# A two-layer decoder trunk on one core: eight landing places for 48 blocks, another order for the second and third phase of a seven-product projection, and attention moved

## The chip, the cores and the metric

The kernel runs on one core of a Trainium2 chip, in one launch. The metric is the device time in microseconds; the profile is of one execution of the same program.

## The reference

Two layers act on x (256 tokens of width 2048, float32), with a memory of 256 tokens beside them. Layer 0 mixes by trailing means over 2, 4, 8 and 16 tokens, layer 1 by block attention; both have a four-head attention into the memory, SiLU gates, an output projection and a layer norm.

```
for i in range(2):
    if i == 1:
        k, v = split(h @ w_kv_shared)
    u = h @ w_in[i]
    branch_in, gate_b, mem_q, gate_m = split(u, [1536, 3072, 3584])
    branch = multiscale_pool(branch_in) if i == 0 else moba_attention(branch_in, k, v)
    mem_o = memory_attention(mem_q, mem, w_mem_kv[i])
    mixed = concat(branch * silu(gate_b), mem_o * silu(gate_m))
    h = layer_norm(ALPHA * h + mixed @ w_out[i], ln_g[i], ln_b[i])
```

## The kernel before

The whole program is one list, `items`. An item is a block of weights, 128 x 1024 values of float32 (512 KB): it is loaded by SyncE into a landing place `raw`, split into a high part `wh` (ScalarE, L73) and a low part `wl = raw - wh` (VectorE, L74), and multiplied on TensorE: high weights with high and low tokens, low weights with high tokens. `run()` walks over the list by hand: in step i it splits item i + 3, issues loads of items ahead, issues item i's products, and then runs what earlier items have put down for this step with `later(n, fn)` (n steps on). There are four buffers each of `raw`, `wh` and `wl`. The first `SHARE` items are loaded `LD0` = 8 items ahead, their landing places being the four `raw` and four pieces of a scratch tile that later becomes `res`; from there on loads go out 4 items ahead into the four `raw`. Each engine's queue runs in order; SyncE's has the loads and the DMA transposes.

An ordinary block makes twelve products of 128x512. The projections of the memory query and memory gate (columns 6 and 7 of `w_in[0]`) are made another way (class `Seven`): with tokens and weights quartered, seven products of half the size instead of eight, as in Strassen's method. Their 28 short blocks of six products each are called p1 to p7, each for the four pieces a, b, c, d: in phase A p1 and p5, in phase B p3, p7, p6 (a3, a7, a6, b3, ...), in phase C p2, p4 (a2, a4, ...). p5, p7, p6 and p4 need a sum of weight blocks first (L729, VectorE). Sums of tokens lie in `zT`. The products gather in the PSUM banks X (`pt`), Y (`o`), V and W (the halves of `s2`, printed as s). Two calls on VectorE and ScalarE make the results: `second` (L710 to L716, after phase B: rows of the memory gate, whose `done2` applies tanh, L287, and a product, L288, then planes of 16 bits, L276, and DMA transposes, L279) and `third` (after phase C: rows of the memory query). Between the short blocks stand ordinary blocks o0 to o23: o0 to o7 a gate of the pool, o8 to o15 and o16 to o23 its inputs. Their results are transposed and joined on ScalarE (L302); from the joined inputs the pool's groups are made in steps on VectorE (L774, L782, L783) and split into `zT`.

Counted from the list's start, p1 of piece a is item 30, o10 42, a3 43, a7 44, o15 54, o16 58, o17 61, o21 73 in both kernels. After item 72 `attend` puts down the memory attention of head pairs 0 and 1: `plan(pair, a, turns, b, c)` sets the step of the scores (a), of four groups of 32x32 transposes (L381), of the splits of the probabilities (b) and of the product with the values (c), counted from there. In that stretch stand the pool's mix with bank o (L822 reads it), the rest of the gates, and then the output projection.

Of the kernel before, what the change touches and what calls it, by code (L numbers as in the profile page):

```python
# [15 lines left out]
ALU = mybir.AluOpType  # L16
# [21 lines left out]
SLOTS = 7  # L38
LD = 4
LD0 = 8  # L40
SHARE = 32
FAR = 6
LP = 3
SEND = 3
# [5 lines left out]
def trunk(ctx: ExitStack, tc: tile.TileContext, a: dict, out: bass.AP):  # L50
    nc = tc.nc
# [16 lines left out]
    def mm(o, l, r, start, stop, **kw):  # L68
        nc.tensor.matmul(o, l, r, start=start, stop=stop, **kw)  # L69
# [7 lines left out]
    items = []  # L77
# [9 lines left out]
    def item(src, cols, consume=None, dst=None):  # L87
        items.append(dict(src=src, cols=cols, consume=consume, dst=dst, cuts=(0, cols)))
# [8 lines left out]
    def later(n, fn):  # L97
        events[now[0] + n].append(fn)
# [111 lines left out]
    def moving(w, src):  # L210

        if len(src.shape) == 3:
            return w.rearrange("p (c k n) -> p k c n", c=2, k=2)
        return w.rearrange("p (k n) -> p k n", n=512)
# [84 lines left out]
    def join(dst, tp, n0=0):  # L299

        n = dst.shape[1]
        nc.scalar.activation(dst.bitcast(U16).rearrange("p n (x h) -> p n h x", h=2), tp[:, n0:n0 + n], AF.Copy)  # L302
# [35 lines left out]
    def heads_tile(name):  # L338
        return sb.tile([P, 4, 2 * T], F32R, name=name)
# [152 lines left out]
    def plan(pr, a, turns, b, c):  # L492

        later(a, pr.a)
        later(a + 1, pr.exps)
        later(a + 2, pr.divide)
        for g, t in enumerate(turns):
            later(t, lambda g=g: pr.turn(g))
        later(b, lambda: pr.b(0))
        later(b + 1, lambda: pr.b(1))  # L500
        later(c, pr.c)
# [119 lines left out]
    class Seven:  # L621
# [46 lines left out]
        def project(self, n1, n2, done1, done2):  # L668
            b, held = {}, {}
            s1, s5 = (lambda: ebuf[:, 0]), (lambda: ebuf[:, 1])  # L670
            e5, e7, e6, e3 = (self.summed(n) for n in range(4))
            a11, a12, a22 = self.tokens(0, 0), self.tokens(8, 0), self.tokens(8, 1)

            def kept(q):
                nm = ("qq", "pp")[q // 2]
                if nm not in held:
                    held[nm] = sb.tile([P, 2 * BLK], F32, name=nm)
                return held[nm][:, q % 2 * BLK:(q % 2 + 1) * BLK]

            def bank(nm):  # L680
                if nm not in b:
                    if nm in "VW":
                        s = ps.tile([P, 2, 512], F32, name="s2")
                        b["V"], b["W"] = s[:, 0], s[:, 1]
                    else:
                        b[nm] = ps.tile([P, 512], F32, name={"X": "pt", "Y": "o"}[nm])
                return b[nm]

            def one(q, src, nm, sta, begin, then=None, make=None):
                def consume(wh, wl):  # L690
                    o = bank(nm)
                    h, l = (moving(w, n1[0]) for w in (wh, wl))
                    for kk in range(2):
                        xh, xl = sta(2 * q + kk)
                        mm(o, xh, h[:, kk], begin and q == kk == 0, False, skip_group_check=not begin)
                        mm(o, xl, h[:, kk], False, False, skip_group_check=not begin)
                    for kk in range(2):
                        mm(o, sta(2 * q + kk)[0], l[:, kk], False, q == 3 and kk == 1, skip_group_check=not begin)
                    if q == 3 and then:
                        then()  # L700
                item(src, BLK, consume)
                it = items.pop()
                if make:
                    it["make"] = make
                return it

            def copy(to, nm):
                return lambda: nc.scalar.activation(to(), b[nm], AF.Copy)

            def second():  # L710
                nc.vector.tensor_add(s5(), s5(), b["V"])
                nc.vector.scalar_tensor_tensor(b["W"], b["X"], -1.0, s5(), op0=ALU.mult, op1=ALU.subtract)
                nc.scalar.activation(s5(), b["X"], AF.Copy)
                nc.vector.scalar_tensor_tensor(b["Y"], b["Y"], -1.0, s5(), op0=ALU.mult, op1=ALU.subtract)
                done2(0, b["Y"])
                done2(1, b["W"])  # L716

            def third():
                nc.vector.tensor_add(b["Y"], b["Y"], s1())
                done1(0, b["Y"])  # L720
                nc.vector.tensor_add(b["V"], b["V"], s5())
                done1(1, b["V"])

            groups = [], [], []
            for q in range(4):
                def added(x, y, to=None):
                    def make(it):
                        r = to() if to else it["raw"]
                        nc.vector.tensor_add(r, x(), y(it))  # L729
                        return r  # L730
                    return make
                k = lambda q=q: kept(q)
                raw = lambda it: it["raw"]
                p1 = one(q, n1[q], "X", a11, True, copy(s1, "X"))
                p5 = one(q, n2[q], "Y", e5, True, copy(s5, "Y"),
                         added(lambda p1=p1: p1["raw"], raw, k))
                groups[0].append((p1, p5))
                p3 = one(q, n2[4 + q], "Y", e3, False)
                last = lambda it, p3=p3: p3["raw"]
                p7 = one(q, n2[q], "V", e7, True, None, added(lambda p3=p3: p3["raw"], raw))  # L740
                p6 = one(q, None, "X", e6, False, second, added(k, last, k))
                groups[1].append((p3, p7, p6))
                p2 = one(q, n1[4 + q], "Y", a12, True)
                p4 = one(q, None, "V", a22, False, third,
                         added(k, lambda it, p2=p2: p2["raw"], k))
                groups[2].append((p2, p4))
            return groups
# [39 lines left out]
    def to_pool(base, where):  # L787
        def then(t, tp, pl):
            i = base
            while i < base + 4:  # L790
                n = min(3 - i % 3, base + 4 - i)
                join((U0, U1)[i // 3 % 2][:, i % 3:i % 3 + n, PAD + t * P:PAD + (t + 1) * P], tp, i - base)
                i += n
                if t == 1 and i % 3 == 0:
                    *steps, spread = pool_group(i // 3 - 1)
                    n, by = 1 + 4 * (i == 12), 1 + (i != 6)
                    for j, fn in enumerate(steps):
                        later(n + j // by, fn)
                    later(n + (len(steps) + by - 1) // by, spread)
        return turned(where, then)  # L800
# [53 lines left out]
    def pool_in(c, where):  # L854
        return collect(proj_n, xT, cols(a["w_in"][0], c), to_pool(4 * c, where))

    def pool_gate(c, where):
        slots = [(4 * c + d + 4) % SLOTS for d in range(4)]
        return collect(proj_n, xT, cols(a["w_in"][0], 3 + c), gates(slots, where))
# [4 lines left out]
    def hooked(it, fn):  # L864

        old = it["consume"]

        def go(*w):
            if old is not None:
                old(*w)  # L870
            fn()
        it["consume"] = go
        return it
# [24 lines left out]
    o = pool_gate(0, in_p) + pool_in(0, in_p) + pool_in(1, in_pp)  # L898
# [10 lines left out]
        p1, p5 = A[q]  # L909
        items += [p1, o[6 + q], p5]  # L910
    (a3, a7, a6), (b3, b7, b6), (c3, c7, c6), (d3, d7, d6) = B
    items += [o[10], a3, a7, o[11], a6, b3, o[12], b7, o[13], b6, o[14], c3, o[15], c7, c6, d3, o[16], d7, d6]
    (a2, a4), (b2, b4), (c2, c4), (d2, d4) = C
    items += [o[17], o[18], a2, a4, b2, o[19], b4, c2, o[20], c4, d2, d4]
    hooked(items[SHARE + 1], pools)
    prs = [MemPair(h0, st, mem_gate) for h0 in (0, 2)]

    def attend(prs=prs):
        plan(prs[0], 7, (10, 11, 12, 13), 14, 20)
        plan(prs[1], 16, (19, 20, 21, 22), 24, 27)  # L920
    after(attend)
    m, g, p, h = mix(0), pool_gate(1, in_q), pool_in(2, in_q), pool_gate(2, in_q)
    items += [o[21], o[22], g[0], *m, g[1], o[23]]
# [54 lines left out]
    for grp in range(3):  # L978
        k = fresh("k", lambda: heads_tile("kk"))
        q = fresh("q", lambda: heads_tile("qq"))  # L980
# [3 lines left out]
        prs = [MobaPair(2 * j, 4 * grp + 2 * j, st) for j in range(2)]  # L984
# [52 lines left out]
    scr = sb.tile([P, 4 * BLK], F32, name="res")  # L1037
    for i in range(SHARE):
        items[i]["lead"] = LD0
# [45 lines left out]
    one = sb.tile([P, BLK], F32R, name="wh", bufs=W_BUFS)[:, :P]  # L1085
# [18 lines left out]
    o = last(0, 0, 512)  # L1104
# [5 lines left out]
    o = last(1, 0, 256)  # L1110
# [6 lines left out]
    o = last(1, 256, 512)  # L1117
# [103 lines left out]
```

## Time and profile before

| what | value |
|---|---|
| time, median of 3 runs | 816.43 us (816.1 to 817.44) |
| profiled execution | 815.97 us |
| its span | 814.2 us |
| mean granted clock of TensorE | 0.992 |
| TensorE (PE) busy | 791.6 us, 97% |
| VectorE (DVE) busy | 618.2 us, 76% |
| ScalarE (ACT) busy | 500.3 us, 61% |
| loads `raw<-in_w_in` | 127 on the page, 512 KB each, median 5.1 us to landing |

PE are the products, PEld their weight loads, which overlap them. A row of the timeline has the start and the time taken in us, the engine, the line, the operation, output <- input, the count, and in brackets the idle time before it with what ended it. A row of the waits has the total, the count and the longest. A row of a stretch has its length, then each engine's busy time, TensorE's granted clock (1.00 is full), the DMA engines' share and GB/s. In the profile the helper's line stands for all its calls, so tiles tell the calls apart.

### The profile page before, as it was taken

How to read it: one execution, taken by the hardware profiler on the slowest of the kernel's cores; microseconds unless marked ns; L12 is line 12 of the kernel's file. 1: busy time of each engine (PE TensorE's matmuls, PEld its weight loads, DVE VectorE, ACT ScalarE, POOL GpSimd, SP SyncE). 2: the span in 40 equal slices, each digit the busy share in tenths (PEclk: the TensorE clock that was granted, in tenths of full speed). 3: DMA queues.
4: the chain of work that ended last, by engine and by line, in shares of the span. 5: the costliest groups of instructions: out<-in, count | busy, mean ns of one | idle time of the engine just before them, and what ended most of it. 6: DMA issues, size and time to landing. Idle time of an engine off the chain costs nothing.

```text
span 814.2 us, 10066 instructions
## 1 busy us (share of the span) xinstructions
PE 791.6 (97%) x3634; PEld 654.5 (80%) x3634; DVE 618.2 (76%) x827; ACT 500.3 (61%) x618; POOL 0.2 (0%) x4
## 2 busy tenths in 40 slices
PE   9999898899989999999999999999999999999997
PEld 6888575678878888888888888888888888888886
DVE  5779787958987875576856796797568955988966
ACT  5667656766666554369967676466765565655531
POOL 0000000000000000000000000000000000000000
PEclk9999999899999999999999999999999999999999
DMA  8984766677666775679995577757865588657922
GB/s 318 383 280 142 216 215 192 183 206 213 178 195 181 257 280 191 199 219 269 267 262 169 175 226 226 169 182 195 235 199 176 189 217 245 179 181 247 319 86 103
DMA packets 122393, 174.25 MB, mean 214 GB/s; under 512 B 58210, under 2 KB 60258, under 8 KB 122082
## 3 DMA queue, kind: packets, MB, share of 16 engines
q1 hardware_dynamic: 121024, 170.16, 69.5%
q10 hardware_dynamic: 1320, 3.46, 1.2%
q8 instruction: 28, 0.46, 0.2%
q14 instruction: 21, 0.17, 0.1%
HBM read 158.39 MB, written 2.10 MB: 197 GB/s over the span
## 4 chain that ended last, share of the span: by engine, by line
PE 85%; ACT 5%; DVE 5%; DMA 3%; issue 3%; SPq 0%; ACTq 0%; DVEq 0%
PE acc L69 76%; PE s L69 3%; PE o L69 3%; ACT wh L73 2%; PE pt L69 2%; DMA raw<-in_w_in 2%; DVE wl L74 2%; DMA raw<-in_w_mv 1%; ACT pl L276 1%; DVE p L381 1%; ACT gate L302 0%; ACT res L302 0%; ACT zT L73 0%; SPq L115 0%; ACT zf L287 0%
## 5 line engine op out<-in xcount | busy, mean ns | idle before, releaser
L74 DVE TENSOR_TENSOR wl<-raw,wh 128x1024 fp32r<-128x1024 f32 (+3 forms) x237 | 281.4, 1200 | 114.7 <-ACT wh L73 112.8
L69 PE MATMUL acc<-wh,xm 128*128 128x512 f32 x1280 | 321.7, 391 | 0.1
L73 ACT ACTIVATE wh<-raw 128x1024 fp32r<-128x1024 f32 (+3 forms) x237 | 240.4, 1036 | 128.0 <-PE acc L69 50.5
L69 PEld LDWEIGHTS acc<-wh,xm 128*128 128x128 f32 x1280 | 240.4, 189 | 50.3 <-ACT wh L73 0.8
L69 PE MATMUL acc<-wl,xm 128*128 128x512 f32 x640 | 174.3, 389 | 0.0
L69 PEld LDWEIGHTS acc<-wl,xm 128*128 128x128 f32 x640 | 120.2, 188 | 25.0
L69 PE MATMUL acc<-wh,zT 128*128 128x512 f32 x448 | 112.0, 390 | 0.0
L69 PEld LDWEIGHTS acc<-wh,zT 128*128 128x128 f32 x448 | 83.7, 188 | 17.1
L69 PE MATMUL acc<-xm 128*128 128x512 f32 x288 | 66.3, 389 | 0.0
L381 DVE STREAM_TRANSPOSE p<-ebuf 32x192 f32<-32x192 f32 (+1 forms) x160 | 63.3, 396 | 2.4
L69 PEld LDWEIGHTS acc<-xm 128*128 128x128 f32 x288 | 53.7, 188 | 10.9
L69 PE MATMUL acc<-wl,zT 128*128 128x512 f32 x224 | 61.0, 389 | 0.0
L69 PEld LDWEIGHTS acc<-wl,zT 128*128 128x128 f32 x224 | 42.1, 188 | 8.7
L74 DVE TENSOR_TENSOR xm<-raw,xm 128x1024 fp32r<-128x1024 f32 (+2 forms) x31 | 35.4, 1154 | 9.5 <-ACT xm L73 9.1
L73 ACT ACTIVATE xm<-raw 128x1024 fp32r<-128x1024 f32 (+2 forms) x31 | 29.9, 994 | 5.8 <-PE acc L69 3.0
L73 ACT ACTIVATE pp<-p 128x384 fp32r<-128x384 f32 (+1 forms) x20 | 11.2, 560 | 31.0 <-DVE p L381 31.0
L73 ACT ACTIVATE zT<-zf 128x512 fp32r<-128x512 f32 (+1 forms) x18 | 10.5, 584 | 27.5 <-DVE zf L387 20.6
L276 ACT ACTIVATE pl<-acc 128x1024 uint16<-128x1024 uint16 x24 | 23.8, 1019 | 4.0 <-PE acc L69 4.0
L69 PE MATMUL acc<-xm,zT 128*128 128x256 f32 (+1 forms) x144 | 22.6, 318 | 0.0
L69 PEld LDWEIGHTS acc<-xm,zT 128*128 128x128 f32 x144 | 20.7, 191 | 1.9
L302 ACT ACTIVATE pl<-ln_g 128x1024 uint16<-128x1024 uint16 x14 | 19.0, 1356 | 0.0
L287 ACT ACTIVATE zf<-acc 128x512 f32<-128x512 f32 x14 | 8.2, 596 | 16.9 <-PE acc L69 16.9
(206 smaller groups left out, 679.6 us busy)
## 6 DMA issues: line engine op xcount, KB each, us to landing
raw<-in_w_in SPq DMA_DIRECT2D x127, 512.0 KB, 5.1
raw<-in_w_out SPq DMA_DIRECT2D x58, 512.0 KB, 3.9
raw<-in_w_sk SPq DMA_DIRECT2D x24, 512.0 KB, 4.3
raw<-in_w_sv SPq DMA_DIRECT2D x24, 512.0 KB, 3.9
raw<-in_w_mv SPq DMA_DIRECT2D x13, 512.0 KB, 6.0
raw<-in_w_mk SPq DMA_DIRECT2D x10, 512.0 KB, 5.3
res<-in_w_mk SPq DMA_DIRECT2D x5, 512.0 KB, 7.1
res<-in_w_in SPq DMA_DIRECT2D x5, 512.0 KB, 7.8
```

The costliest lines, as they stand in the source:

```text
L69: nc.tensor.matmul(o, l, r, start=start, stop=stop, **kw)
L73: nc.scalar.activation(hi, src, AF.Copy)
L74: nc.vector.tensor_sub(lo, src, f(hi))
L276: nc.scalar.activation(pls[0][:, t], src.bitcast(U16).rearrange("p (n h) -> p h n", h=2), AF.Copy)
L287: nc.scalar.activation(src, acc, AF.Tanh, scale=0.5)
L302: nc.scalar.activation(dst.bitcast(U16).rearrange("p n (x h) -> p n h x", h=2), tp[:, n0:n0 + n], AF.Copy)
L381: nc.vector.transpose(self.p[32 * g:32 * g + 32, h * self.n:(h + 1) * self.n], self.e[32 * h:32 * h + 32, g * self.n:(g + 1) * self.n])
```

## The change

- `SHARE` goes from 32 to 48: items 32 to 47 are loaded eight ahead into eight landing places. With it the pool's scratch (`pools`, four memsets, and the tile `res` in the landing places' memory) comes at item 49 instead of 33.
- p3 begins its bank instead of adding to p5's. `second` is cut in two. One step after the last p6, s5 becomes -X - s5 (L711 of the changed kernel). One step after the last p7, `results` takes bank Y and then V from that sum, with the gate's tanh and product behind each, and only then copies X for the third phase.
- The last pair of phase B is d6, d7 instead of d7, d6. Ahead of phase C stand o17, o18, o19 instead of o17, o18, and the order is a2, a4, b2, b4, o20, c2, c4, d2, d4 instead of a2, a4, b2, o19, b4, c2, o20, c4, d2, d4.
- The steps of the pool's first group are put four items later.
- The first pair's scores, turns and first splits come one item later, the second pair's product two items later.

```diff
-SHARE = 32
+SHARE = 48
...
             def second():
-                nc.vector.tensor_add(s5(), s5(), b["V"])
-                nc.vector.scalar_tensor_tensor(b["W"], b["X"], -1.0, s5(), op0=ALU.mult, op1=ALU.subtract)
+                nc.vector.scalar_tensor_tensor(s5(), b["X"], -1.0, s5(), op0=ALU.mult, op1=ALU.subtract)
+
+            def results():
+                nc.vector.tensor_sub(b["Y"], s5(), b["Y"])
+                done2(0, b["Y"])
+                nc.vector.tensor_sub(b["W"], s5(), b["V"])
+                done2(1, b["W"])
                 nc.scalar.activation(s5(), b["X"], AF.Copy)
-                nc.vector.scalar_tensor_tensor(b["Y"], b["Y"], -1.0, s5(), op0=ALU.mult, op1=ALU.subtract)
-                done2(0, b["Y"])
-                done2(1, b["W"])
...
-                p3 = one(q, n2[4 + q], "Y", e3, False)
+                p3 = one(q, n2[4 + q], "Y", e3, True)
...
-                p7 = one(q, n2[q], "V", e7, True, None, added(lambda p3=p3: p3["raw"], raw))
-                p6 = one(q, None, "X", e6, False, second, added(k, last, k))
+                p7 = one(q, n2[q], "V", e7, True, lambda: later(1, results), added(lambda p3=p3: p3["raw"], raw))
+                p6 = one(q, None, "X", e6, False, lambda: later(1, second), added(k, last, k))
...
-                    n, by = 1 + 4 * (i == 12), 1 + (i != 6)
+                    n, by = {3: 5, 12: 5}.get(i, 1), 1 + (i != 6)
...
-    items += [... c6, d3, o[16], d7, d6]
+    items += [... c6, d3, o[16], d6, d7]
...
-    items += [o[17], o[18], a2, a4, b2, o[19], b4, c2, o[20], c4, d2, d4]
+    items += [o[17], o[18], o[19], a2, a4, b2, b4, o[20], c2, c4, d2, d4]
...
-        plan(prs[0], 7, (10, 11, 12, 13), 14, 20)
-        plan(prs[1], 16, (19, 20, 21, 22), 24, 27)
+        plan(prs[0], 8, (11, 12, 13, 14), 15, 20)
+        plan(prs[1], 16, (19, 20, 21, 22), 24, 29)
```

SyncE's queue around items 28 to 61, first as it was. The first row are items 28 to 31, the pair on qq the transposes of the memory keys, the first pair on p those of the pool's gate, the second those of the pool's first input.

```order
L113 DMA res<-in_w_in 128x2x512 x4
L279 DMA_TRANSPOSE qq<-pl 128x8x128 x2
L113 DMA raw<-in_w_in 128x2x512 x11
L279 DMA_TRANSPOSE p<-pl 128x8x128 x2
L113 DMA raw<-in_w_in 128x2x512 x15
L279 DMA_TRANSPOSE p<-pl 128x8x128 x2
```

The first pair on p stood behind the load of o10 (item 42). Now:

```order
L113 DMA res<-in_w_in 128x2x512 x4
L113 DMA raw<-in_w_in 128x2x512
L279 DMA_TRANSPOSE qq<-pl 128x8x128 x2
L113 DMA raw<-in_w_in 128x2x512 x3
L113 DMA res<-in_w_in 128x2x512 x4
L113 DMA raw<-in_w_in 128x2x512 x4
L113 DMA res<-in_w_in 128x2x512 x2
L279 DMA_TRANSPOSE p<-pl 128x8x128 x2
L113 DMA res<-in_w_in 128x2x512
L113 DMA raw<-in_w_in 128x2x512 x11
L279 DMA_TRANSPOSE p<-pl 128x8x128 x2
```

The loads of a3, a7 and o11 have moved ahead of the first pair on p, and six of the loads ahead of it go to the scratch (res) instead of a `raw`.

VectorE's queue from the end of phase B to a4's low split, as it was (the first two rows are the low splits of o18 and a2; qq<-qq,raw is a4's sum; L774, L782 and L783 are the pool's first group):

```order
L74 TENSOR_TENSOR wl<-raw,wh 128x1024 x2
L711 TENSOR_TENSOR ebuf<-ebuf,s_822 128x512
L712 SCALAR_TENSOR_TENSOR s_822<-pt,ebuf 128x512
L714 SCALAR_TENSOR_TENSOR o<-o,ebuf 128x512
L288 SCALAR_TENSOR_TENSOR zf<-zf,o 128x512
L288 SCALAR_TENSOR_TENSOR zf<-zf,s_822 128x512
L774 TENSOR_TENSOR res<-res 128x3x256
L782 TENSOR_TENSOR res<-res,ln_g 128x3x256
L729 TENSOR_TENSOR qq<-qq,raw 128x1024
L783 TENSOR_TENSOR res<-res 128x3x256
L74 TENSOR_TENSOR wl<-raw,wh 128x1024
L74 TENSOR_TENSOR wl<-qq,wh 128x1024
```

And as it is now (the row ahead of L714 is a2's low split, the two sums qq<-qq,raw are a4's and b4's):

```order
L711 SCALAR_TENSOR_TENSOR ebuf<-pt,ebuf 128x512
L74 TENSOR_TENSOR wl<-raw,wh 128x1024
L714 TENSOR_TENSOR o<-ebuf,o 128x512
L288 SCALAR_TENSOR_TENSOR zf<-zf,o 128x512
L716 TENSOR_TENSOR s_810<-ebuf,s_810 128x512
L288 SCALAR_TENSOR_TENSOR zf<-zf,s_810 128x512
L731 TENSOR_TENSOR qq<-qq,raw 128x1024
L74 TENSOR_TENSOR wl<-raw,wh 128x1024
L74 TENSOR_TENSOR wl<-qq,wh 128x1024
L731 TENSOR_TENSOR qq<-qq,raw 128x1024
L776 TENSOR_TENSOR res<-res 128x3x256
L784 TENSOR_TENSOR res<-res,ln_g 128x3x256
```

The first result stands behind a2's split and frees bank o before the second is begun; the pool's steps have moved from ahead of a4's sum to behind b4's.

TensorE's queue at the second pair's product (o<-pp,vv), as it was: pt, o and s are the pool's second mix, acc the gate's blocks behind it.

```order
L69 MATMUL o<-zT,wh 128x256 x6
L69 MATMUL o<-zT,wl 128x256 x3
L69 MATMUL s_1924<-zT,wh 128x256 x6
L69 MATMUL s_1924<-zT,wl 128x256 x3
L69 MATMUL o<-pp,vv 128x256 x12
L69 MATMUL acc<-wh,xm 128x512 x8
```

And now:

```order
L69 MATMUL s_1917<-zT,wh 128x256 x6
L69 MATMUL s_1917<-zT,wl 128x256 x3
L69 MATMUL acc<-wh,xm 128x512 x8
L69 MATMUL acc<-wl,xm 128x512 x4
L69 MATMUL acc<-wh,xm 128x512 x8
L69 MATMUL acc<-wl,xm 128x512 x4
L69 MATMUL o<-pp,vv 128x256 x12
```

Two ordinary blocks have come between the mix and the product.

More of the change, by code (lines that the diff above doesn't have):

```diff
@@ L911, in trunk @@
     (a3, a7, a6), (b3, b7, b6), (c3, c7, c6), (d3, d7, d6) = B
-    items += [o[10], a3, a7, o[11], a6, b3, o[12], b7, o[13], b6, o[14], c3, o[15], c7, c6, d3, o[16], d7, d6]
+    items += [o[10], a3, a7, o[11], a6, b3, o[12], b7, o[13], b6, o[14], c3, o[15], c7, c6, d3, o[16], d6, d7]
     (a2, a4), (b2, b4), (c2, c4), (d2, d4) = C
-    items += [o[17], o[18], a2, a4, b2, o[19], b4, c2, o[20], c4, d2, d4]
+    items += [o[17], o[18], o[19], a2, a4, b2, b4, o[20], c2, c4, d2, d4]
     hooked(items[SHARE + 1], pools)
```

## The prediction

> **What bounds the kernel now.** I read the head of the page first, then busy time by stage, then what TensorE's weight loads (PEld) waited for.
>
> ```profile
> span 814.2 us, 10066 instructions
> PE 791.6 (97%) x3634; PEld 654.5 (80%) x3634; DVE 618.2 (76%) x827; ACT 500.3 (61%) x618; POOL 0.2 (0%) x4
> ```
>
> ```profile
> core 0: us, PE busy (x) PEld busy (x) DVE busy (x) ACT busy (x) POOL busy (x), PEclk, DMA share, GB/s
> 66.00:132.00 66.00, 61.19 (x255) 46.49 (x254) 55.31 (x56) 42.52 (x50) 0.00 (x0) 1.00 0.69 208
> 132.00:163.50 31.50, 25.59 (x97) 19.94 (x97) 26.95 (x27) 21.67 (x26) 0.00 (x0) 0.89 0.59 168
> 163.50:262.00 98.50, 94.27 (x456) 79.68 (x455) 78.47 (x113) 65.03 (x88) 0.00 (x0) 0.98 0.70 194
> 262.00:800.00 538.00, 538.00 (x2504) 450.77 (x2503) 402.37 (x562) 325.81 (x404) 0.00 (x0) 1.00 0.71 212
> 63.70:86.30 22.60, 21.51 (x94) 17.14 (x93) 22.38 (x30) 15.44 (x20) 0.00 (x0) 1.00 0.50 161
> ```
>
> TensorE is the bound: from 262 to 800 us it has no idle time, so a microsecond gained earlier reaches the end whole. What can be gained lies before: 4.8 us idle from 66 to 132, 5.9 in the next stage, 4.2 after it, and the time in which the clock was below 1.00. The last row says that VectorE is full from 63.7 to 86.3; nothing that comes earlier for it can move that stretch.
>
> The waits that follow are nearly all of short blocks (banks o, s, pt), whose weights ScalarE and VectorE have to add and split. I go through the change in the order of time.
>
> **Part 1, eight landing places.** Removed is the wait for loads; no instruction is added. These rows are of SyncE, then of the three engines.
>
> ```profile
> 82.92 4.33 SPq L279 DMA_TRANSPOSE p<-pl  x2
> 87.36 34.21 SPq L113 DMA_DIRECT2D raw<-in_w_in  x15
> ...
> 86.27 1.22 DVE L729 TENSOR_TENSOR pp<-raw 128x1024 f32<-128x1024 f32 x1
> 89.62 0.76 PEld L69 LDWEIGHTS o<-wh,zT 128*128 128x128 f32 x4 [1.11 <-ACT wh L73]
> 92.03 1.06 ACT L73 ACTIVATE wh<-raw 128x1024 fp32r<-128x1024 f32 x1 [1.98 <-DMA raw<-in_w_in]
> 98.03 0.76 PEld L69 LDWEIGHTS s<-wh,zT 128*128 128x128 f32 x4 [1.91 <-ACT wh L73]
> 106.28 2.99 ACT L73 ACTIVATE wh<-raw 128x1024 fp32r<-128x1024 f32 x3 [3.40 <-DMA raw<-in_w_in]
> ```
>
> And these are PEld's waits by cause from 105 to 127 us (the first two) and from 127 to 132.1:
>
> ```profile
> PEld s L69 <- DVE wl L74: 0.7, 1, 0.7
> PEld s L69 <- ACT wh L73: 0.4, 1, 0.4
> ...
> PEld pt L69 <- DVE wl L74: 0.9, 1, 0.9
> PEld s L69 <- DVE wl L74: 0.5, 1, 0.5
> PEld pt L69 <- ACT wh L73: 0.3, 1, 0.3
> PEld s L69 <- ACT wh L73: 0.3, 1, 0.3
> ```
>
> a3's load is the first behind the transposes of 82.92: issued at 87.36, it landed at 92.03, 4.7 us later. Now a3's, a7's and o11's loads stand ahead of the transposes. Up to 86.27 nothing moves (VectorE full). Then d's sum for p5 ends at 87.5; ScalarE is free, its split takes 1.06, and the matmul starts at 88.7 instead of 89.62. a3's split need not wait until 92.03, so a7, behind o10, a3 and two pairs of gate joins on ScalarE (1.4 us each, row of 130.00 below), starts at 95.3 instead of 98.03: 2.7 us earlier. The load waited for at 106.28 is issued some ten microseconds earlier too, which takes most of b7's waits (0.4 and 0.7): 3.5. d6 and d7 change places; of their four waits (2.0 us) I keep 0.6 for d7's low half, since VectorE does d6's split first. o17, which starts at 132.12 (row below), starts at 127.7: **4.4 us**. Bounds: nothing if VectorE's row were as full from 86 to 132 as before it (it is busy 84% from 66 to 132), and the 4.8 us that TensorE is idle there.
>
> Cover: the four loads behind the transposes (b3, o12, b7, o13) now go out in one row from 87.4 on; at the 4.7 us above and 2.5 us more for each that follows (512 KB at the stage's 208 GB/s) the last is there by 99.6, and wanted at 101 or later.
>
> **Part 2, second results, three ordinary blocks, pool steps.**
>
> ```profile
> 130.00 1.39 ACT L302 ACTIVATE res<-p 128x768 uint16<-128x768 uint16 x2
> 132.12 1.78 PEld L69 LDWEIGHTS acc<-wh,xm 128*128 128x128 f32 x8
> ...
> 135.75 0.68 DVE L711 TENSOR_TENSOR ebuf<-ebuf,s 128x512 f32<-128x512 f32 x1
> 138.63 0.60 ACT L287 ACTIVATE zf<-o 128x512 f32<-128x512 f32 x1 [0.77 <-DVE o L714]
> 139.98 2.01 ACT L276 ACTIVATE pl<-zf 128x1024 uint16<-128x1024 uint16 x2 [0.27 <-DVE zf L288]
> 140.00 0.77 PEld L69 LDWEIGHTS o<-wh,xm 128*128 128x128 f32 x4 [2.47 <-DVE zf L288]
> 140.46 0.95 DVE L774 TENSOR_TENSOR res<-res 128x768 f32<-128x768 f32 x1
> ...
> 143.64 1.06 ACT L73 ACTIVATE wh<-qq 128x1024 fp32r<-128x1024 f32 x1 [0.70 <-DVE qq L729]
> ...
> 144.74 0.76 PEld L69 LDWEIGHTS s<-wh,xm 128*128 128x128 f32 x4 [3.50 <-ACT wh L73]
> 163.53 0.64 PEld L69 LDWEIGHTS acc<-wh,xm 128*128 128x128 f32 x3
> ```
>
> Eight weight loads of an ordinary block take 1.78 us, so its twelve take 2.7 and a short block's six 1.36. From o17 (132.12) to o21 (163.53) are 31.4 us, of which four ordinary and eight short blocks are 21.8: 9.6 are lost, in a2's wait of 2.47, a4's of 3.50 and the clock behind them.
>
> The arithmetic of the results is three vector operations before and after (0.7 each), and one ScalarE copy in both, now off the path; its worth is the order. Worked forward: o17 starts at 127.7. d7's high split stands on ScalarE at 124.6; behind it come joins, o18, joins, o19, a2 (1.06 for a split, 1.4 for two joins): 7.0 us, so a2's ends at 131.6; its low split on VectorE ends near 133, and the results begin at 133.5. Subtraction 0.7, tanh 0.6, L288 0.7 and hand-offs: bank o is free at 135.7. TensorE needs it at 127.7 + 3 x 2.7 = 135.9. **a2's wait of 2.47 goes.**
>
> What is late next is a4. The second result runs to 137.0; then ScalarE has, ahead of a4's split, the copy (0.6), the two planes (the 2.01 of the row, which stood behind it before) and b2's split (1.06): a4's split is at 140.3, its matmul at 141.4, while a2 ends at 137.2. A wait of 4.2 us, no shorter than the 3.50 before. From there VectorE is the bound: a4, b2, b4 follow each other without an ordinary block to cover their sums, and the first pool group's four steps (0.95 each, moved here from ahead of a4) lie between them. From a4's low split at 141.5 to d4's there are ten operations of 1.15 to 1.2 and these four, 15.5 us; d4's low half starts at 158.3 and o21 at 158.7. That is 31.0 us from o17 against 31.4: **0.4 us**. Most of what the three blocks cover comes back as waits of a4, b4, c4 and d4. Bounds: 9.6 us if none of these waits came, and a loss of 2.4 if every sum, split and product of the four pairs ran one behind the other (1.3 + 1.1 + 1.6 + 1.36 each, with o20 24.2 from 141.4).
>
> **Part 3, attention.**
>
> ```profile
> 181.28 0.30 PEld L69 LDWEIGHTS s<-kk,qq 128*128 128x128 f32 x2 [0.92 <-ACT qq L310]
> 182.54 1.24 PEld L69 LDWEIGHTS s<-kk,qq 128*128 128x128 f32 x10 [0.96 <-DVE qq L311]
> 220.45 1.61 PEld L69 LDWEIGHTS o<-pp,vv 128*128 128x128 f32 x12
> 242.07 2.64 PEld L69 LDWEIGHTS o<-pp,vv 128*128 128x128 f32 x12 [3.15 <-issue]
> ```
>
> The first pair's scores go behind one more ordinary block, 2.7 us, against waits of 0.92 and 0.96: **1.9 us**. The second pair's last product waits 3.15 us for the bank o that the pool's mix has just filled and VectorE not yet read; moved behind two ordinary blocks (5.4 us) it finds it free. Behind that wait the same twelve loads take 2.64 us against 1.61. The clock's rows say why:
>
> ```profile
> 142.53:145.95 3.42, 1.19 (x4) 0.67 (x4) 3.42 (x4) 2.72 (x4) 0.00 (x0) 1.00 1.21 213
> 145.95:149.36 3.41, 2.62 (x6) 2.15 (x7) 3.41 (x4) 1.37 (x2) 0.00 (x0) 0.50 0.28 81
> 149.36:152.77 3.41, 3.41 (x9) 2.65 (x9) 3.34 (x4) 2.83 (x4) 0.00 (x0) 0.50 0.73 225
> 238.11:241.52 3.41, 1.01 (x9) 0.81 (x7) 2.27 (x4) 2.74 (x4) 0.00 (x0) 1.00 1.04 323
> 241.52:244.93 3.41, 2.83 (x13) 2.86 (x14) 2.89 (x6) 1.05 (x2) 0.00 (x0) 0.50 1.11 261
> ```
>
> A stretch with TensorE busy 1.0 to 1.2 us of 3.41 is followed by one or two at half the clock. So the moved product gains 3.15 + 1.03 = **4.2 us**. Its users: the gated output follows three microseconds behind it on VectorE and ScalarE, and the out projection's second block, which reads it, now stands three ordinary blocks (8.1 us) behind. Were that cover gone, it would cost one for one. The Trainium skill (TensorE: Matmul & The Clock Gate, section on the HAM clock gate) gives one idle window of about 3.4 us as what sends the clock to half. By that rule a wait of 3.15 us would have cost no clock, this term would be 3.1, and the sum's end 806.6. The row of 238.11 disagrees: it was not idle throughout, and half speed followed. The measurement decides.
>
> a4's wait of 4.2 us will bring the half clock again; I cost it at nothing, because TensorE waits for VectorE from there to o21.
>
> **Sum.** 4.4 + 0.4 + 1.9 + 4.2 = 10.9 us off the profiled execution's 815.97 (span 814.2 and 1.8 around it): 805.1. The median of the runs is 816.43, 0.46 higher; I say **805.5**. The memsets of the pool's scratch, which move by 16 items, and the later loads I cost at nothing: both are behind TensorE's ordinary blocks, and VectorE only gains room where it was full.
>
> **Rivals.**
> *The landing places bring nothing.* VectorE, full until 86.3, stays the bound, and everything up to o17 stands where it stood. For it: the 22.38 of 22.60. Against it: ScalarE's waits of 1.98 and 3.40 for loads. Without the 4.4: 809.9.
> *Phase three runs free.* VectorE makes up its row while o17 to o19 run, and b4, c4 and d4 find their splits done. Against it: VectorE was busy 27 of 31.5 us in a stage that was 31.4 long. Without these three pairs of waits (some 4.9 us): 800.6.
> *The clock stays at half.* a4's wait sends it down, and short blocks that wait for VectorE keep it there: 145.95 to 149.36 was 77% busy and did not bring it back. From a4 on TensorE's 12.2 us of work to o21 would take 24.5: o21 at 165.9, 7.2 us later than I say, end at 812.7. If it stayed low further, each two microseconds cost one more, and from about 177 us on the kernel would be slower than before; that is the way to the other side. Against it: 149.36 to 152.77 was fully busy and full speed followed, and a half clock itself raises the busy share. The Trainium skill (same page, section on HAM oscillation) describes such a kernel that falls back at each of its waits; no run here shows more than two slow stretches in a row.
>
> **How the numbers follow.** My forecast 0.72; places without effect 0.10; free phase three 0.08; clock 0.10 (half of it slower than before, some of it level). 0.2%, 1.6 us, is about what a measurement of this kernel can tell. Faster by more: 0.93; within: 0.02; slower: 0.05. The range goes from 800.5 (free phase three) to 810.0 (no effect of the places) and leaves out the clock's case and slips of several terms together, under 2 in 10.
>
> **What would show it.** Right: no wait for raw at ScalarE from 87 to 107; o17 near 127.7; no wait at a2; a wait of about four microseconds at a4, by the split of qq, then half the clock; o21 near 158.7; no wait at the scores, nor at the second pair's product, and the clock at 1.00 around it. Wrong: loads late behind the transposes, gate joins that ScalarE waits for, or a clock below 1.00 beyond o21.

## The result, and the profile after

The changed kernel takes 809.12 us (median of four runs, 807.82 to 810.55) against 816.93 (816.1 to 817.69) for the kernel before on the same chip: a ratio of 0.9905, 95% interval 0.9881 to 0.9929. A second set, six runs of it beside eleven of the kernel before, gave 809.08 against 815.37, 0.9924 (0.9908 to 0.994). So it is faster by 0.6 to 1.2%, 3.6 us behind the forecast of 805.5 and inside its range.

The page's head, and then busy time by stage as in the prediction (TensorE, its loads, VectorE, ScalarE, GpSimd, clock, DMA share, GB/s):

```profile
span 806.3 us, 10062 instructions
PE 787.4 (98%) x3634; PEld 651.8 (81%) x3634; DVE 617.7 (77%) x827; ACT 498.8 (62%) x618; POOL 0.2 (0%) x4
```

```profile
66.00:126.40 60.40, 58.87 (x253) 46.66 (x252) 54.62 (x55) 42.40 (x50) 0.00 (x0) 1.00 0.72 210
126.41:157.27 30.86, 25.22 (x98) 18.46 (x97) 25.93 (x26) 20.92 (x26) 0.00 (x0) 0.94 0.58 167
157.27:256.00 98.73, 95.52 (x469) 80.72 (x468) 80.08 (x115) 64.44 (x89) 0.00 (x0) 1.00 0.70 198
256.00:800.00 544.00, 542.50 (x2544) 454.85 (x2542) 407.85 (x577) 326.43 (x406) 0.00 (x0) 1.00 0.70 211
```

Of the 4.8 us that TensorE was idle up to o17, 1.5 are left. In the third phase it is idle for 5.6. In the third row 3.2 us are idle at full clock. The last row, full before, now has 1.5 us idle. What these idle times are say the waits of PEld from 60 to 300 us (total, count, longest):

```profile
PEld s L69 <- ACT wh L73: 6.3, 4, 4.3
PEld s L69 <- DVE wl L74: 4.2, 6, 1.6
PEld acc L69 <- DVE zf L288: 3.6, 1, 3.6
PEld o L69 <- ACT wh L73: 1.5, 2, 1.3
PEld acc L69 <- DVE zT L74: 1.1, 1, 1.1
PEld o L69 <- DVE wl L74: 1.0, 2, 0.5
```

The waits of the scores (0.9 and 1.0) and of the second pair's product (3.1) are gone. Two are new, both of blocks that gather in acc: 3.6 us for the gate's product L288, and 1.1 us for zT. The timeline of PEld at the places that the prediction named, and at the two new waits:

```profile
126.41 1.80 PEld L69 LDWEIGHTS acc<-wh,xm 128*128 128x128 f32 x8
...
134.69 0.78 PEld L69 LDWEIGHTS o<-wh,xm 128*128 128x128 f32 x4
...
140.19 1.06 PEld L69 LDWEIGHTS s<-wh,xm 128*128 128x128 f32 x4 [4.25 <-ACT wh L73]
...
157.27 1.80 PEld L69 LDWEIGHTS acc<-wh,xm 128*128 128x128 f32 x8
...
176.87 1.61 PEld L69 LDWEIGHTS s<-kk,qq 128*128 128x128 f32 x12
...
210.60 1.69 PEld L69 LDWEIGHTS acc<-wh,xm 128*128 128x128 f32 x8 [3.63 <-DVE zf L288]
...
239.74 1.61 PEld L69 LDWEIGHTS o<-pp,vv 128*128 128x128 f32 x12
...
284.90 1.00 PEld L69 LDWEIGHTS acc<-wh,zT 128*128 128x128 f32 x5 [1.14 <-DVE zT L74]
```

In order: o17 at 126.41, a2 without a wait, a4 with 4.25, o21 at 157.27, the scores whole, the block behind L288, the second product whole, and a block of the output projection that waits for zT.

Both traces have the same 3634 weight loads, so they can be lined up by number. Where the 7.9 us came from, stage by stage (o21 is load 621 counted from 0; 840, 1040 and 1300 fall at 202, 245 and 299 us of the changed kernel):

| stage | before | after | gain | forecast |
|---|---|---|---|---|
| start to piece c's p5 (load 339) | 82.79 | 82.08 | 0.7 | 0 |
| to o17 | 49.33 | 44.34 | 5.0 | 4.4 |
| o17 to o21 | 31.41 | 30.85 | 0.6 | 0.4 |
| o21 to load 840, the scores in it | 46.11 | 44.38 | 1.7 | 1.9 |
| to load 1040, the second product in it | 44.32 | 43.40 | 0.9 | 4.2 |
| to load 1300 | 53.25 | 54.27 | -1.0 | 0 |
| from there to load 3600 | 495.51 | 495.51 | 0 | 0 |

The forecast missed 3.3 us in one stage and 1.0 behind it. The first row varied from 81.90 to 83.08 in the other profiles of kernels that have the eight places, so its 0.7 lies within the scatter.

### The profile page after: what moved, and what is told of

It is laid out like the page before. It is cut to its first block, busy times and chain, and to the rows that moved or that the text cites. A ratio compares the mean times of both kernels' runs of the same rounds, so it can differ in the third digit from the quotient of the medians.

```text
span 806.3 us, 10062 instructions
## 1 busy us (share of the span) xinstructions
PE 787.4 (98%) x3634; PEld 651.8 (81%) x3634; DVE 617.7 (77%) x827; ACT 498.8 (62%) x618; POOL 0.2 (0%) x4
## 4 chain that ended last, share of the span: by engine, by line
PE 84%; DVE 6%; ACT 3%; issue 3%; DMA 3%; SPq 0%; ACTq 0%; DVEq 0%
PE acc L69 76%; PE s L69 3%; DVE wl L74 3%; PE o L69 3%; PE pt L69 2%; ACT wh L73 2%; DMA raw<-in_w_out 1%; DMA raw<-in_w_mk 1%; DMA raw<-in_w_in 1%; DVE pp L731 1%; DVE res L776 0%; DVE res L785 0%; DVE zf L288 0%; DVE zT L74 0%; ACT pl L276 0%
## 5 line engine op out<-in xcount | busy, mean ns | idle before, releaser
L74 DVE TENSOR_TENSOR wl<-raw,wh 128x1024 fp32r<-128x1024 f32 (+2 forms) x231 | 274.1, 1199 | 109.3 <-ACT wh L73 106.9
L73 ACT ACTIVATE wh<-raw 128x1024 fp32r<-128x1024 f32 (+2 forms) x231 | 233.7, 1034 | 112.1 <-PE acc L69 47.4
L74 DVE TENSOR_TENSOR wl<-res,wh 128x1024 fp32r<-128x1024 f32 x18 | 21.9, 1224 | 5.4 <-ACT wh L73 4.8
L73 ACT ACTIVATE wh<-res 128x1024 fp32r<-128x1024 f32 x18 | 18.8, 1058 | 6.9 <-DMA res<-in_w_mk 3.1
```

What stands on the lines that cost most here:

```text
L73: nc.scalar.activation(hi, src, AF.Copy)
L74: nc.vector.tensor_sub(lo, src, f(hi))
```

## The experiments

Each kernel was timed beside the kernel before on the same chip; ratios are to that. Profiles are of one execution each. By their times alone, the edits to single parts are not told apart from the changed kernel (0.9905 and 0.9924, with intervals that overlap theirs), except for the kernel without the places; what one of them does is read from the stages of its profile. The two combinations at the end are told apart from the changed kernel timed beside them.

**The places alone.** The kernel before with one line changed:

```diff
-SHARE = 32
+SHARE = 48
```

> The kernel before with SHARE = 48 alone (the eight landing places for items 32 to 47, nothing else). Theory: the places are worth what the step to o17 showed. Before, o17 starts 49.3 us after the short block at 82.79; in the changed kernel 44.3 us after it: 4.4 to 5.0 us. Phase C stays as it was (31.4 us from o17 to o21), the waits at the scores and at the second pair's product stay: about 812.2 us. Rival one (VectorE is full there, the places help nothing): 816.9. Rival two (the time is won but given back, since what follows is bound by its own chain of results, not by when o17 starts): o17 early, phase C longer, 815 or more.

Measured: 809.88 us, 0.993 (0.9904 to 0.9955), as fast as the whole change and 2.3 us less than expected. The six runs go from 807.75 to 812.0, and the profile is of one of the longest, 811.73. Load 339 to o17 took 44.41 us. o17 to o21 took 29.60, with the old order, against 31.41 before. In before TensorE was busy for all of 153 to 166 us, having worked 6.8 us at half the clock from 145.95; here the slow stretch began at 135.9, within a4's wait. The second product's wait stood as before:

```profile
237.51 2.02 PEld L69 LDWEIGHTS o<-pp,vv 128*128 128x128 f32 x12 [3.17 <-issue]
```

Ahead of that the time won was given back in part: from o21 to load 840 this kernel took 48.85 us against 46.11 before, since the scores waited 2.10 and 0.96 us and half the clock followed for 3.4 us. In the changed kernel, whose scores come one block later, this stage has no wait.

**All but the places.** The changed kernel with SHARE at 32 again.

> The changed kernel with SHARE = 32 (everything but the landing places). Theory: the terms add, so it loses what the places gave, 4.4 to 5.0 us: 813.8 us, with o17 near 132 and phase C near 31. Rival (the wait of 3.6 us on L288 near 207 us came because TensorE was early): that wait shrinks or goes when TensorE is later, and the kernel ends at 810 to 811.

Measured: 814.36, 0.9987 (0.997 to 1.0004). Load 339 to o17 took 49.32, as before. So the places carry the change, and without them everything else together is worth no more than 0.3%. L288 was waited for again (3.58 us at 215.37) with TensorE five microseconds later, so that wait does not come from the early start; the rival is out. o17 to o21 took 29.95.

**First pair's scores back.**

```diff
-        plan(prs[0], 8, (11, 12, 13, 14), 15, 20)
+        plan(prs[0], 7, (10, 11, 12, 13), 14, 20)
```

> The changed kernel with the first pair's steps as before (scores at 7, turns 10 to 13, first split 14); the second pair's product stays at 29. Theory: the new wait of 3.6 us (ordinary block behind L288, near 207 us) comes from the first pair's turns and splits, moved one step later into the steps in which the second pair's maxima and the pool's steps stand on VectorE. So it goes, and the scores' waits of 0.92 and 0.96 come back: 3.6 - 1.9 = 1.7 us faster than the changed kernel, about 807.4. Rival (the wait has another cause, TensorE being early against VectorE's work): it stays, the scores' waits come back too, 811.

Measured: 808.27, 0.9911 (0.9879 to 0.9944). L288's wait is gone, loads 840 to 1040 took 39.88 instead of 43.40. The scores wait again, and half the clock followed them for 3.4 us, so that o21 to load 840 took 48.00 instead of 44.38. The mechanism was as expected, the gain of 1.7 us was not: what came back at the scores is as much as what went at L288.

```profile
175.21 0.30 PEld L69 LDWEIGHTS s<-kk,qq 128*128 128x128 f32 x2 [1.21 <-ACT qq L310]
176.47 1.78 PEld L69 LDWEIGHTS s<-kk,qq 128*128 128x128 f32 x10 [0.96 <-DVE qq L311]
```

**Scores late, turns back.**

```diff
-        plan(prs[0], 8, (11, 12, 13, 14), 15, 20)
+        plan(prs[0], 8, (10, 11, 12, 13), 14, 20)
```

> The changed kernel with the first pair's scores one step later (8), as in the change, but turns and splits where they were before (10 to 13, 14). Theory: both waits go, that of the scores and that on L288: 809.1 - 3.6 = 805.5 us. Rival (VectorE's amount of work up to L288 is what counts, not its order): the wait near 207 stays within 1 us of 3.6, about 809.

Measured: 810.01, 0.9932 (0.9909 to 0.9955). L288's wait stayed, 3.72 us. The order behind the scores doesn't set it; the rival was right.

**The pool's second group later**, to take work from ahead of L288:

```diff
-                    n, by = {3: 5, 12: 5}.get(i, 1), 1 + (i != 6)
+                    n, by = {3: 5, 6: 6, 12: 5}.get(i, 1), 1 + (i != 6)
```

> The changed kernel with the steps of the pool's second group put five items later on VectorE, so that they follow the gate's product L288 for which an ordinary block waits at 210.6 us. Theory (that wait of 3.6 us is VectorE's amount of work between the first pair's scores and L288, 28.5 us without idle): the wait goes, the stretch around it takes 39.8 us instead of 43.4, and the kernel takes 805.5 us. Rival (the order behind the scores sets it, through the transposes and the tanh on ScalarE ahead of L288): the wait stays within half a microsecond and the time at 809. Given back in part, if the moved steps make the splits of the pool's mix late: a new wait of one to three microseconds between 220 and 245, 807 to 808.

Measured: 808.17, 0.992 (0.9905 to 0.9935). PEld's waits from 60 to 300 us that bear on it:

```profile
PEld acc L69 <- ACT wh L73: 1.4, 1, 1.4
PEld acc L69 <- DVE zf L288: 1.3, 1, 1.3
...
PEld acc L69 <- DVE zT L74: 1.0, 1, 1.0
PEld pt L69 <- DVE zT L74: 0.9, 1, 0.9
PEld acc L69 <- DVE wl L74: 0.8, 1, 0.8
```

2.3 us of L288's wait are gone, so VectorE's amount of work ahead of it is a cause. 1.9 us come back at 228 to 231, where an ordinary block now waits for its low split and the mix (pt) for that group, and 1.4 at 273. The time is the 807 to 808 that was expected for this case, and not 805.5. Work moved off one full stretch was waited for in the next.

**Two ordinary blocks ahead of the third phase.**

```diff
-    items += [o[17], o[18], o[19], a2, a4, b2, b4, o[20], c2, c4, d2, d4]
+    items += [o[17], o[18], a2, a4, b2, o[19], b4, o[20], c2, c4, d2, d4]
```

> The changed kernel with the order o17, o18, a2, a4, b2, o19, b4, o20, c2, c4, d2, d4: two ordinary blocks ahead of the third phase instead of three. Theory (VectorE is the bound from a4 to o21, so the third block only moves idle time from a2 to a4): o17 to o21 stays between 30 and 31.5 us, a2 waits 1.5 to 2.5 us again and a4 less than 4.2, time 808.5 to 810. Rival (the third block hides a2's wait for good): o17 to o21 takes 33 us, time 811.

Measured: 809.55, 0.9934 (0.9919 to 0.9949); o17 to o21 took 30.73. a2 waits 1.95 and a4 2.38: the third block had only moved idle time from one to the other.

**The pool's first steps out of the third phase.** The same line with `{3: 13, 12: 5}`.

> The changed kernel with the steps of the pool's first group put eight items later still, out of the third phase. Theory of the prediction (VectorE, with these four steps of 0.95 us between the sums, is the bound from a4 to o21): o21 comes 2.5 to 3.5 us earlier, and 806 us if nothing waits for the moved steps. Rival (the chain of sum, split and product through ScalarE sets the pace, and the steps lie in VectorE's gaps): o21 moves by less than 0.7 us, time 808 to 810.

Measured: 807.12, 0.9898 (0.9878 to 0.9918). o17 to o21 took 28.05, 2.8 less.

**The planes held two items,** by a new argument to the helper that sends the gate's results:

```diff
-                later(1, lambda: planes(t, src))
+                later(1 + hold, lambda: planes(t, src))
...
-            later(SEND + gate, lambda: send(t))
+            later(SEND + gate + hold, lambda: send(t))
...
-                            gates(None, in_p, lambda: [(h0, mem_gate(h0)) for h0 in (0, 2)]))
+                            gates(None, in_p, lambda: [(h0, mem_gate(h0)) for h0 in (0, 2)], 2))
```

> The changed kernel with the planes, sends and joins of the gate's results put two items later, so that a4's split on ScalarE no longer stands behind the planes (2.0 us). Theory of the prediction (a4's wait of 4.2 us is ScalarE's row: copy, planes, b2's split): a4 waits 2.2 to 2.9 us instead of 4.25; since VectorE is then the bound, o21 comes 0.5 to 1.4 us earlier, 807.5 to 808.5. Rival (a4's sum on VectorE ends last): a4's wait stays over 3.7 us, and the time at 809.

Measured: 808.89, 0.9929 (0.9912 to 0.9945). a4's wait fell as the theory has it, and o17 to o21 took 28.80, 2.05 less, where 0.5 to 1.4 were expected; in the time nothing of it is seen.

```profile
138.27 0.76 PEld L69 LDWEIGHTS s<-wh,xm 128*128 128x128 f32 x4 [2.40 <-ACT wh L73]
```

In this profile and in the one of the experiment before it L288's wait was followed by half the clock (3.4 and 6.8 us of it), in that of the changed kernel not; more on that at the end.

**The changed kernel again.**

> The changed kernel itself, beside the others of this call: 809 us as before. The ordinary block's wait for L288 takes 3.6 us again, whatever the grid of the clock's windows does; whether half the clock follows it depends on where the wait lies in a window.

Measured: 809.08 (808.0 to 811.68), the second set above. L288's wait was 3.55 us.

**The second product back.**

```diff
-        plan(prs[1], 16, (19, 20, 21, 22), 24, 29)
+        plan(prs[1], 16, (19, 20, 21, 22), 24, 27)
```

> The changed kernel with the second pair's product put back by two items, in front of the two ordinary blocks. Theory of the prediction (the product waits for bank o, 3.15 us, and half the clock may follow, 1.03 us): its wait of 3 us is there again, the stretch around it is 3 to 4.5 us longer; the wait of 1.1 us near 283 us (the output projection's second block) is gone, since it stands later; 811 to 812.5 us. Rival (what the product loses there is slack that the later wait near 283 takes back): 809 to 810.

Measured: 810.36, 0.9935 (0.9921 to 0.9949), 1.3 us behind the changed kernel in the same set, which these intervals do not tell from nothing. The theory was half wrong, on the size:

```profile
210.71 2.42 PEld L69 LDWEIGHTS acc<-wh,xm 128*128 128x128 f32 x8 [3.95 <-DVE zf L288]
...
237.88 1.49 PEld L69 LDWEIGHTS o<-pp,vv 128*128 128x128 f32 x12 [1.71 <-issue]
```

With TensorE held up by L288 27 us before, the product waits 1.71 us and not 3.15: likely two waits in a row share what VectorE is behind, which no run tested. And the wait near 283 us is gone with the move undone. In the three profiles with the product at its old place there is no such wait; of the eleven with it moved, ten have it, with 0.55 to 1.14 us. So the move has its part in it.

**Both third-phase edits, and the scores back.** The last two single edits of that phase with `plan(prs[0], 7, (10, 11, 12, 13), 14, 20)`.

> Three single edits together: the pool's first steps out of the third phase, the planes of the gate's results held two items, and the first pair's scores back at item 7. Theory (each of the three waits has its own cause on VectorE or ScalarE, and they add): o17 to o21 takes 26.5 to 27.5 us, the scores wait 2.2 us and half the clock follows, L288 is not waited for: 804.5 to 805.5 us. Rival (what is gained in the third phase makes VectorE's full stretch meet the scores or L288 earlier, and the wait comes back there): 807.

Measured: 805.23 (804.91 to 806.44), 0.9874 (0.9859 to 0.9889); the changed kernel beside it had 809.08 and 0.9924 (0.9908 to 0.994). o17 to o21 took 26.49. The scores waited 1.3 and 1.0 us, as in the run with the scores alone back, but no slow stretch followed in this profile, and L288 wasn't waited for. The time is as expected, its parts not quite: the half clock that was expected stayed away, and 1.7 us of new waits for zT came at 162 and 163, where the pool's mix waits for the group whose steps were moved. This version beats both kernels.

**Both third-phase edits, scores late, second group later:**

```diff
-                    n, by = {3: 5, 12: 5}.get(i, 1), 1 + (i != 6)
+                    n, by = {3: 13, 6: 5, 12: 5}.get(i, 1), 2
```

> The pool's first steps out of the third phase, the planes held two items, the scores left at item 8, and the pool's second group four items later and two steps an item, so that its first stands behind L288. Theory: o17 to o21 takes 26.5 to 27.5 us; L288 is waited for 1.3 us at most, without half the clock behind it; the mix at 228 us finds its group split: 801.5 to 803.5 us. Rival (VectorE's work from the scores to the mix is the bound, and what is taken from ahead of L288 is waited for at the mix): waits of 2 us or more at 225 to 232, 804.5 to 806.5.

Measured: 805.65 (804.04 to 806.0), 0.9873 (0.9857 to 0.9888). o17 to o21 took 26.00 and L288 wasn't waited for. Between 222 and 227 us there were waits of 1.0 us in all. The larger loss stood where neither theory looked, at a split in the output projection, with 3.4 us of half the clock behind it:

```profile
268.45 2.62 PEld L69 LDWEIGHTS acc<-wh,zT 128*128 128x128 f32 x8 [2.13 <-ACT wh L73]
```

## Why the prediction was right, and where it was not

**The range held with some luck.** The 809.12 measured lie near its end of 810.0, and near the 809.9 that the prediction gave for places that bring nothing: the time alone would not have told the two apart, the first two experiments do. Part 3 brought 1.6 us of the 6.1 forecast, and 0.7 from the first row and 0.6 more from part 1 made up for some of it.

**Part 1 held.** 4.4 us forecast, 4.99 measured, 4.92 with the places alone. ScalarE's waits for loads from 87 to 107 us are gone; what is left there is for sums (3.3, 1.9 and 1.8 us in total, by line L731). The rival "places bring nothing" is out. Two details were off. The terms of the sum do not make 4.4: the 3.5 and what the 0.6 leaves of the four waits' 2.0 make 4.9. And d6 ahead of d7 brought nothing of it, since the places alone, with the old order, took as long. Whether it is the loads' order in SyncE's queue or the number of places that counts was not taken apart.

**Part 2 had the mechanism right; that its size agreed is luck.** a2's wait went, a4's was 4.25 against 4.2, o17 to o21 30.85 against 31.0. That a4 waits for ScalarE's row is shown by the held planes (4.25 to 2.40), that VectorE paces the rest by the pool's steps (2.8 us for four of 0.95 taken out). Together the two took 30.85 to 26.49 and 26.00: in this stage they nearly add. The third ordinary block is worth nothing there. But the gain of 0.6 against 0.4 proves little: the seven profiles with this order of the phase took 29.95 to 31.02, and the old order took 31.41 before and 29.60 with the places alone. Whether the new order is worth anything by itself is not shown.

That half the clock costs nothing while TensorE waits for VectorE agrees with the profile with the first pair's scores back: it had 6.8 us of it in this stage and took 30.56, the changed kernel 3.4 us and 30.85. In the kernel before it had cost something, because TensorE was the one that was late: it had no more waits from 147 us to o21. With the places alone the slow stretch fell into a4's wait, and the stage was 1.8 us shorter. This reading rests on one profile of each. The rival of a clock that stays low is out: in no profile of the third phase were there more than two windows of 3.4 us at half. So is the free third phase: TensorE still waited 4.0 us in all for the split halves of b4, c4 and d4. The loss of 2.4 among this part's bounds does not follow from the 24.2 us given beside it, which would make it 6.5; neither was reached.

**Part 3 is the step that failed**, the sentence that the first pair's scores behind one more block gain 1.9 us. The waits at the scores did go. But it asked only what TensorE waits for ahead of the scores, and not what follows from them on VectorE. PEld's row of before for the block that waits now:

```profile
215.01 1.77 PEld L69 LDWEIGHTS acc<-wh,xm 128*128 128x128 f32 x8
```

And VectorE's, first L288 in before, then the stretch up to it in after:

```profile
214.23 1.28 DVE L288 SCALAR_TENSOR_TENSOR zf<-zf,acc 128x512 f32<-128x512 f32 x2
```

```profile
181.34 1.22 DVE L352 TENSOR_REDUCE nb<-s 128x4 f32<-128x1024 f32 x1
...
185.78 1.22 DVE L74 TENSOR_TENSOR wl<-raw,wh 128x1024 fp32r<-128x1024 f32 x1 [1.87 <-ACT wh L73]
...
209.87 1.28 DVE L288 SCALAR_TENSOR_TENSOR zf<-zf,acc 128x512 f32<-128x512 f32 x2
```

The first of L288's two instructions frees a bank 0.73 us after its start (210.60 after 209.87). In before that is 214.96, and TensorE came for it at 215.01: the slack was 0.05 us, and no wait showed. From the scores' first weight load to this block are 33.73 us in both kernels (181.28 to 215.01, 176.87 to 210.60). VectorE is busy for 26.06 of the 28.53 us between its reduction and L288; the only idle times over 0.15 us are 1.87 (the row) and 0.16. So this chain is nearly as long as VectorE's work. TensorE's own work in it was 33.73 less the 0.96 that it waited inside the scores, 32.8; one block later it is 2.72 less, 30.1. The difference to 33.73 is 3.7, and the wait is 3.63. So by a row that can be read in the profile before, the move had to lose 1.7 us: 1.9 less 3.6. Undone, in the third experiment, it changed next to nothing in the profile (3.6 us longer up to load 840, half the clock included, and 3.5 shorter behind it), and the times of 808.27 and 809.12 are not told apart. Either way the 1.9 did not come.

The product's term of 4.2 was of the right size by itself: with the scores at item 7, loads 840 to 1040 took 44.63 with the product at its old place (first experiment) and 39.88 moved (third), 4.75, the clock's share included. But behind load 1040, 1.7 us came back (54.96 against 53.25). With L288's wait ahead of it the two stages from load 840 to 1300 took 100.32 with the move undone, against 97.67 and 99.97 in the changed kernel's two profiles.

The 1.0 us given back near 283 is the other half of the miss. The cover that the prediction named held: the second block of the output projection started without a wait, five microseconds after its zT was split. The block that waits stands 35 us later and reads the pool's last mix (L824):

```profile
243.37 0.69 DVE L74 TENSOR_TENSOR zT<-zf,zT 128x512 fp32r<-128x512 f32 x1 [0.70 <-ACT zT L73]
...
249.36 1.77 PEld L69 LDWEIGHTS acc<-wh,zT 128*128 128x128 f32 x8
...
283.77 0.48 DVE L824 SCALAR_TENSOR_TENSOR zf<-s,psc,gate 128x256 f32<-128x256 f32 x1
284.17 1.02 DVE L74 TENSOR_TENSOR zT<-zf,zT 128x512 fp32r<-128x512 f32 x2
```

What the prediction lacked is what follows there: the loads of the projection come late (ScalarE waits four times for raw<-in_w_out from 245 to 295 us, 3.2 us in all, against 0.5 before), and VectorE has low splits of these blocks ahead of L824. Undoing the move takes the wait away; why these loads are late there, and more so in the two fastest versions (5.6 and 5.1 us), wasn't isolated.

## What to carry to other kernels

A wait that a profile doesn't show may be one block away: before moving a step later, measure from its start to each later event that it leads to on the other engine, and compare with the time at which the first engine comes for it; 0.05 us of slack look like no dependence at all. Two gains that stood on the same busy engine did not add up here, where it was full between them; those of the third phase, each with its own cause, nearly did. Timing single parts showed that one constant carried nearly all of this change. And a stage that comes out as forecast in one profile proves little until other profiles show how far it varies.

## What the hardware showed beyond that

TensorE's clock changes on a grid of 3.41 us, whose place differs from execution to execution. The same kernel with the same wait for L288, first the profile of after, then that of its second set (length, TensorE busy, ..., clock):

```profile
205.41:208.82 3.41, 1.98 (x9) 1.31 (x7) 3.38 (x6) 0.83 (x4) 0.00 (x0) 1.00 0.70 217
208.82:212.23 3.41, 1.63 (x7) 1.36 (x8) 3.41 (x5) 3.41 (x9) 0.00 (x0) 1.00 0.37 121
212.23:215.65 3.42, 3.42 (x17) 2.81 (x16) 3.33 (x8) 3.16 (x4) 0.00 (x0) 1.00 0.54 158
```

```profile
207.68:211.09 3.41, 1.02 (x5) 0.52 (x3) 3.38 (x5) 1.87 (x9) 0.00 (x0) 1.00 0.50 162
211.09:214.50 3.41, 2.67 (x6) 2.17 (x7) 3.37 (x6) 3.41 (x5) 0.00 (x0) 0.50 0.46 156
214.50:217.92 3.42, 3.42 (x9) 2.67 (x8) 3.33 (x8) 2.22 (x3) 0.00 (x0) 0.50 0.72 178
```

Split over two windows the wait cost its own length; within one it cost 6.8 us at half the clock besides, and loads 840 to 1040 took 46.12 us instead of 43.40. Over the windows from 100 to 300 us of all fourteen profiles, full speed was lost after each of the 20 with TensorE busy 1.48 us or less, after none with 1.88 or more, and after some between; from half speed it came back after each with 2.83 or more, and after none with 2.79 or less. The Trainium skill (TensorE: Matmul & The Clock Gate, section on the HAM clock gate) gives about 3.4 us as the window, which the grid bears out, and an idle window as the condition; here windows with up to 1.48 us of work were already too idle. The kernel before ran between 812.4 and 818.7 us over all sets; that this scatter is the grid's place is likely by these rows, but no run tested it.
